# Half of the output mix by plain products, gate's residual moved into the feed-forward, embeddings split in two

## The chip, the core and the metric

The kernel runs on one core of a Trainium2 chip. The metric is the device time of one execution in microseconds (us), from runs without a profile. Its engines work side by side, each through its own list in order: TensorE (PE, matmuls; PEld loads its weights), VectorE (DVE), ScalarE (ACT), GpSimd (POOL) and SyncE (SP). SP, POOL and ACT also start DMA transfers, which all stand in that engine's list: a transfer that must wait holds what is behind it.

## The reference

One layer of a trunk with 512 tokens and 2048 channels, in float32:

```python
proj = h @ w_in                               # q, k, v of head groups A and B
oa   = banded_attention(qa, ka, va, ...)      # group A, windowed
ob   = dilated_attention(qb, kb, vb)          # group B, three dilations
ya, yb = rms_norm(oa, gn_a), rms_norm(ob, gn_b)
mix  = concatenate([ya, yb]) @ w_o
h    = layer_norm(ALPHA * h + mix, ln1_g, ln1_b)
ff   = square(relu(h @ w1)) @ w2              # 8192 wide
ple  = (p @ w_ple) * sigmoid(h @ w_ple_gate)  # per-layer embedding (256 wide) and its gate
h    = layer_norm(ALPHA * h + ff + ple, ln2_g, ln2_b)
```

## The kernel before

A float32 product is made of three matmuls of a reduced type: every operand is split in a high part (ScalarE, copy with rounding) and a low part (VectorE, the difference), and TensorE adds hi x hi, hi x lo and lo x hi. A weight tile is 128x1024 floats (512 KB); its parts are `wh` (L86) and `wl` (L87). `put` does the same for the other operand and makes the pair `s1h`, `s1l` and so on.

The large products use Strassen's scheme (`strassen`): over token halves (`th`) and quarters of the weight matrix, 7 products p of 4 steps k each take the place of 8. A step is 12 matmuls of 128x512, a call is 28 steps or 336 matmuls. The operands of the 7 products are sums of quarters: on the weight side VectorE makes them (L518, L523, L535, L536 and others), on the token side the `factors` (tiles `qh`, loaded from DRAM; in the feed-forward `qs`). Three PSUM chains `a`, `b`, `c` collect products; `quarters` puts them together to result quarters (th, nh) and hands each to a function: `mixed`, `gated`, `squared` or `last_sum`.

The stages, in order: input projection and attention (to about 500 us in the trace), with its last pieces between the embeddings `embed(0)` to `embed(3)` (48 matmuls for each two, p x w_ple, stored in `ple_d`); RMSNorm (`rms_stats`, `rms_scale`: the factor `r` by small VectorE ops L296 to L302, spread by TensorE L306, copied L322, applied L326, stored in `y_d`); the mix in two calls (`c` = 0, 1), each for half of the output columns; the first layer norm (`norm_rows`: rows L641, transposes `pt` L629, factors `ha`, stored in `h_d`, and `z_d` for the rows themselves); gate in two calls; eight chunks of the first feed-forward product (`squared`, factors stored in `s_d`); the second feed-forward product; the last layer norm. `gated` (L685 to L696) takes each quarter of gate: it loads the embedding `pl`, the normalized rows `zn` and LayerNorm's two rows `gb`, broadcast over all partitions, through ACT's list, and computes sig x ple + ALPHA x (zn x gain + bias), which goes to `z_d` as the residual for the last norm.

The program is written in this order of calls; a scheduler sorts the instructions of each engine by its own estimates, and tiles are drawn from rings (tags) with a fixed number of buffers: a new tile waits until the last reader of the buffer's former tile is done. Rings that matter here: "g" (4 buffers), "q" (2), "r" (4), "k" (4) and "wh", "wl" (3 each).

## Time and profile before

| | us |
|---|---|
| median of 3 runs (lowest, highest) | 2283.46 (2281.01, 2284.67) |
| the profiled execution | 2283.15 |
| its span, first to last instruction | 2281.4 |
| TensorE busy | 2156.5 (95%) |
| VectorE busy | 1663.9 (73%) |
| ScalarE busy | 1074.0 (47%) |

TensorE's mean granted clock is 0.977 of full speed. In the rows below, "L566" is a line of the kernel, "`b<-wh,s5h`" an instruction that writes tile `b` from `wh` and `s5h`, and a bracket at a row's end the idle time of the engine before it with what ended it. TensorE is busy nearly all the time, so the stretches in which it is not are what there is to read.

### The profile page before, as it was taken

To read this page: it belongs to the slowest core of one execution; us is meant where nothing else is said; L and a number is where in the kernel's file an instruction comes from. 1 tells how busy PE (TensorE), PEld (TensorE's weight loads), DVE (VectorE), ACT (ScalarE), POOL (GpSimd) and SP (SyncE) were. 2 spreads that over 40 slices of the span, in tenths; PEclk is the share of its full clock that TensorE was granted. 3 is DMA by queue.
4 is the path that set the end of the run, shared out by engine and by line. 5 is a ranking of instruction groups with operands and counts; after the bars stand their busy time and mean duration, and the time that the engine had idled before them with its cause. 6 is when DMAs were issued, how large, how long until landed. Compare 5 with 4: busy or idle time off the path is not lost.

```text
span 2281.4 us, 25611 instructions
## 1 busy us (share of the span) xinstructions
PE 2156.5 (95%) x9528; PEld 1743.6 (76%) x9528; DVE 1663.9 (73%) x1890; ACT 1074.0 (47%) x1300; POOL 112.9 (5%) x188
## 2 busy tenths in 40 slices
PE   8999999997997979899999999999899999999995
PEld 7888888875776757688887888877687787787784
DVE  7675655546988878777776876877777776777787
ACT  5454333344544634354554555455455455555331
POOL 0000000000001000000000000000011011101000
PEclk9999999998998989999999999999999999999998
DMA  6212322237767786655565565567669779679562
GB/s 226 77 65 83 114 72 83 78 105 282 245 203 244 268 260 204 196 205 197 197 231 171 189 231 174 195 231 249 191 197 267 192 202 278 176 216 285 170 242 102
DMA packets 132285, 433.01 MB, mean 190 GB/s; under 512 B 13600, under 2 KB 22832, under 8 KB 132160
## 3 DMA queue, kind: packets, MB, share of 16 engines
q1 hardware_dynamic: 93984, 300.19, 39.2%
q0 software_dynamic: 25760, 93.43, 14.3%
q10 hardware_dynamic: 12416, 37.75, 4.9%
q8 instruction: 75, 1.23, 0.2%
q14 instruction: 50, 0.41, 0.1%
HBM read 352.68 MB, written 78.64 MB: 189 GB/s over the span
## 4 chain that ended last, share of the span: by engine, by line
PE 71%; DMA 11%; DVE 11%; issue 4%; ACT 2%; DVEq 0%; SPq 0%; ACTq 0%
PE a L569 9%; PE a L566 9%; PE a L568 9%; PE u L93 6%; PE u L94 6%; PE u L95 6%; PE b L569 5%; PE b L568 5%; PE b L566 5%; DVE wl L87 4%; DMA wr<-in_w 3%; DMA qs<-s_d 2%; DMA gb<-in_lnb 2%; PE c L569 2%; PE c L566 2%
## 5 line engine op out<-in xcount | busy, mean ns | idle before, releaser
L86 ACT ACTIVATE wh<-wr 128x1024 fp32r<-128x1024 f32 (+1 forms) x400 | 415.3, 1042 | 562.0 <-PE a L568 222.1
L87 DVE TENSOR_TENSOR wl<-wr,wh 128x1024 fp32r<-128x1024 f32 (+1 forms) x400 | 477.4, 1198 | 223.3 <-ACT wh L86 218.5
L86 ACT ACTIVATE wh<-wk 128x1024 fp32r<-128x1024 f32 x160 | 169.6, 1060 | 201.7 <-PE a L568 99.1
L87 DVE TENSOR_TENSOR wl<-wk,wh 128x1024 fp32r<-128x1024 f32 x160 | 194.5, 1220 | 67.8 <-ACT wh L86 67.1
L93 PE MATMUL u<-xh,wh 128*128 128x512 f32 x576 | 227.6, 395 | 5.9 <-ACT xh L73 5.9
L95 PE MATMUL u<-xh,wl 128*128 128x512 f32 x576 | 226.0, 392 | 0.0
L94 PE MATMUL u<-xl,wh 128*128 128x512 f32 x576 | 225.5, 391 | 0.0
L518 DVE TENSOR_TENSOR wk<-wr,wk 128x1024 f32<-128x1024 f32 x80 | 97.8, 1223 | 91.0 <-DMA wr<-in_w 86.8
L566 PE MATMUL b<-wh,s5h 128*128 128x512 f32 x320 | 130.5, 408 | 24.6 <-ACT wh L86 13.6
L569 PE MATMUL b<-wl,s5h 128*128 128x512 f32 x320 | 130.6, 408 | 12.9 <-DVE wl L87 12.9
L569 PE MATMUL c<-wl,s2h 128*128 128x512 f32 x320 | 128.4, 401 | 9.8 <-DVE wl L87 9.7
L569 PE MATMUL a<-wl,s1h 128*128 128x512 f32 x320 | 128.9, 403 | 8.2 <-DVE wl L87 8.2
L566 PE MATMUL a<-wh,s1h 128*128 128x512 f32 x320 | 128.3, 401 | 4.5 <-ACT wh L86 2.3
L568 PE MATMUL b<-wh,s5l 128*128 128x512 f32 x320 | 129.8, 406 | 1.9 <-DVE s5l L445 1.9
L569 PE MATMUL a<-wl,s7h 128*128 128x512 f32 x320 | 126.8, 396 | 4.0 <-DVE wl L87 4.0
L566 PE MATMUL a<-wh,s7h 128*128 128x512 f32 x320 | 127.0, 397 | 3.2 <-ACT wh L86 1.7
L93 PEld LDWEIGHTS u<-xh,wh 128*128 128x128 f32 x576 | 108.7, 189 | 27.6 <-ACT xh L73 5.9
L569 PE MATMUL b<-wl,s3h 128*128 128x512 f32 x320 | 126.7, 396 | 2.5 <-DVE wl L87 2.4
L566 PE MATMUL a<-wh,s6h 128*128 128x512 f32 x320 | 125.5, 392 | 3.2 <-DVE zl L743 2.1
L566 PE MATMUL c<-wh,s2h 128*128 128x512 f32 x320 | 127.8, 399 | 0.0
L568 PE MATMUL c<-wh,s2l 128*128 128x512 f32 x320 | 127.6, 399 | 0.0
L568 PE MATMUL b<-wh,s3l 128*128 128x512 f32 x320 | 127.4, 398 | 0.0
(234 smaller groups left out, 4548.7 us busy)
## 6 DMA issues: line engine op xcount, KB each, us to landing
wr<-in_w SPq DMA_DIRECT2D x196, 512.0 KB, 4.0
wr<-in_w_in SPq DMA_DIRECT2D x64, 512.0 KB, 3.8
wq<-in_w SPq DMA_DIRECT2D x64, 512.0 KB, 3.9
wk<-in_w POOLq DMA_DIRECT2D x64, 512.0 KB, 4.8
qs<-s_d SPq DMA_DIRECT2D x56, 512.0 KB, 4.9
z_d<-ev POOLq DMA_DIRECT2D x42, 512.0 KB, 7.2
s_d<-f POOLq DMA_DIRECT2D x32, 512.0 KB, 5.2
wg<-in_w SPq DMA_DIRECT2D x32, 512.0 KB, 4.7
```

Of the source, the lines that this page charges most:

```text
L86: nc.scalar.activation(hi, t, AF.Copy)
L87: nc.vector.tensor_tensor(lo, t, hi.bitcast(F32), op=ALU.subtract)
L93: nc.tensor.matmul(o, wh, ah, start=start, stop=False)
L94: nc.tensor.matmul(o, wh, al, start=False, stop=False)
L95: nc.tensor.matmul(o, wl, ah, start=False, stop=stop)
L518: nc.vector.tensor_tensor(t4[k], get(b21, k, 2, "r"), t2[k], op=ALU.subtract)
L566: nc.tensor.matmul(o, sh[:, i, x], wh[:, c], start=first and k == 0 and j == 0, stop=False, skip_group_check=skip)
L568: nc.tensor.matmul(o, sl[:, i, x], wh[:, c], start=False, stop=False, skip_group_check=skip)
L569: nc.tensor.matmul(o, sh[:, i, x], wl[:, c], start=False, stop=k == 3 and j == 1, skip_group_check=skip)
```

## The change

Three edits go together, and their places in the order of the instructions follow below.

1. Half 0 of the mix is made by `plain`, an ordinary product of 4 pieces of 96 matmuls (384 instead of 336), on the unsummed factors `s1`, `s7` (blocks 0 and 2; the second is stored under the key 21), `s2`, `s4`. The first piece needs head group A alone and is interleaved with attention's end; the second needs group B. The sums that half 1 still needs are made meanwhile (`y_sums`). The PSUM pool of attention is split in two sides so that four banks live on.
2. `embed(2)` and `embed(3)` come after the mix; the split embedding input `ph`, `pl` is loaded and made again in buffers of `s1l`, results go through ring "q".
3. `gated` keeps the sigmoid and stores it in `g_d`. The rest (`residual`) is spread over the eight chunks of the first feed-forward product, a quarter in each: loads by SP in step 7 of 28, scaling in the 11th, sums and a store by POOL in the 14th.

```diff
-    embed(0)
-    V = v_split(V)
-    embed(1)
-    hd.turn()
-    embed(2)
-    ssB = hd.values(V, ssB, oB)
-    rB = rms_stats(ssB)
-    embed(3)
-    rms_scale(oB, rB, 8)
+    for g in range(2):
+        put(sy[g], 1, y_block(g, 0))
+        put(sy[g], 7, y_block(g, 2), 21)
+    embed(0, p_hl, bank, "g")
+    V = v_split(V)
+    embed(1, p_hl, bank, "g")
+    hd.turn()
+    o = [bank() for _ in range(NQ)]
+    plain(0, 0, o, range(2))
+    ssB = hd.values(V, ssB, oB)
+    plain(0, 0, o, range(2, 3))
+    rB = rms_stats(ssB)
+    plain(0, 0, o, range(3, 4))
+    rms_scale(oB, rB, 8)
...
+    for g in range(2):
+        put(sy[g], 2, y_block(g, 1))
+        put(sy[g], 4, y_block(g, 3))
...
+    def plain(nh, kh, o, steps=range(4)):
+        for k in steps:
+            wh, wl = w_split(w_load(w_o[0, 2 * kh + nh, k], "r"))
+            for j in range(2):
+                i = 2 * (k % 2) + j
+                c = slice(j * S, (j + 1) * S)
+                for t in range(NQ):
+                    ah, al = sy[k // 2][((1, 2), (21, 4))[t // 2][kh]]
+                    x = slice((t % 2) * P, (t % 2 + 1) * P)
+                    first, end = kh == k == j == 0, kh == j == 1 and k == 3
+                    nc.tensor.matmul(o[t], ah[:, i, x], wh[:, c], start=first, stop=False)
+                    nc.tensor.matmul(o[t], al[:, i, x], wh[:, c], start=False, stop=False)
+                    nc.tensor.matmul(o[t], ah[:, i, x], wl[:, c], start=False, stop=end)
...
+    plain(0, 1, o, range(2))
+    y_sums(0)
+    plain(0, 1, o, range(2, 4))
+    y_sums(1)
+    plain_out(0, o)
...
+    plain(1, 0, o)
+    for g in range(2):
+        x, y = y_block(g, 0), y_block(g, 2)
+        nc.vector.tensor_tensor(x, x, y, op=ALU.subtract)
+        put(sy[g], 7, x)
+    plain(1, 1, o)
+    plain_out(1, o)
...
-    for c in range(2):
-        def mixed(th, nh, y, c=c):
...
-            if c == 1 and all((th, m) in zs for m in range(4)):
-                norm_rows(th)
-        strassen(lambda k, q, c=c: w_o[c, q, k], sy, quarters(mixed, {(1, 0): "k"} if c else {}),
-                 between=mid if c == 0 else {}, steps=ENDS if c else FIRST1)
+    def mixed(th, nh, y):
...
+        if (th, 5 - n) in zs:
+            norm_rows(th)
+            if th == 1:
+                ph, pl = (s_tile(f"p{c}", "s1l", (P, 2, S), R32) for c in "hl")
+                r = pair("pr", "q")
+                nc.sync.dma_start(r, pT.rearrange("k p s -> p k s"))
+                nc.scalar.activation(ph, r, AF.Copy)
+                nc.vector.tensor_tensor(pl, r, ph.bitcast(F32), op=ALU.subtract)
+                rest.append([(ph[:, k], pl[:, k]) for k in range(2)])
+
+    strassen(lambda k, q: w_o[1, q, k], sy, quarters(mixed, {(1, 0): "k"}), steps=ENDS)
+    for g in range(2, 4):
+        embed(g, rest[0], pt_bank, "q")
...
         def gated(th, nh, g, c=c):
-            n = 2 * c + nh
-            e = pair("pl", "g")
-            nc.scalar.dma_start(e, ple_d[th, n])
-            z = pair("zn", "g")
-            nc.scalar.dma_start(z, z_d[th, n])
-            gb = pair("gb", "g")
-            nc.scalar.dma_start(gb, bass.AP(tensor=lnb.tensor, offset=lnb.offset + n * S, ap=[[0, P], [D, 2], [1, S]]))
             nc.scalar.activation(g, g, AF.Sigmoid)
-            nc.vector.tensor_tensor(g, g, e, op=ALU.mult)
-            for i in range(2):
-                nc.vector.scalar_tensor_tensor(z[:, i], z[:, i], ALPHA, gb[:, 0], op0=ALU.mult, op1=ALU.mult)
-                nc.vector.scalar_tensor_tensor(z[:, i], gb[:, 1], ALPHA, z[:, i], op0=ALU.mult, op1=ALU.add)
-            nc.vector.tensor_tensor(g, g, z, op=ALU.add)
-            nc.scalar.dma_start(z_d[th, n], g)
+            nc.scalar.dma_start(g_d[th, 2 * c + nh], g)
...
+    def residual(th, n):
+        t = {}
+        def load():
+            for name, d in (("zn", z_d), ("sg", g_d), ("pl", ple_d)):
+                t[name] = pair(name, "g")
+                nc.sync.dma_start(t[name], d[th, n])
+            t["gb"] = pair("gb", "g")
+            nc.sync.dma_start(t["gb"], bass.AP(tensor=lnb.tensor, offset=lnb.offset + n * S,
+                                               ap=[[0, P], [D, 2], [1, S]]))
...
     for n in range(NFC):
+        mid = dict(at[False]) if n == NFC - 1 else {}
+        for i, step in zip((6, 10, 13), residual(n % 2, n // 2)):
+            mid[i] = mid.get(i, []) + [step]
```

The names below are the program's, "waits" names the queue or engine whose semaphore is waited for, and lines of the changed kernel are those of its own text. TensorE at the end of attention, before: the last embedding's matmuls (`u`), the spread of RMSNorm's factor (`s`), and the mix's first matmul:

```order
2352 L93 MATMUL u<-wh,ph 128x512
2353 L94 MATMUL u<-wl,ph 128x512
2354 L95 MATMUL u<-wh,pl 128x512
2355 L306 MATMUL s<-ident,r 128x128 [waits DVE_49,PE_49]
2356 L306 MATMUL s<-ident,r 128x128 x3
2357 L566 MATMUL a<-wh,s1h 128x512 [waits Activation_49]
```

The same place now: the end of the plain product over head group A (`s7`, L458 to L460), the spread, and the plain product over group B (`s2`):

```order
2405 L458 MATMUL u<-wh,s7h 128x512
2406 L459 MATMUL u<-wh,s7l 128x512
2407 L460 MATMUL u<-wl,s7h 128x512
2408 L307 MATMUL s<-ident,r 128x128 [waits DVE_49,PE_49]
2409 L307 MATMUL s<-ident,r 128x128 x3
2410 L458 MATMUL u<-wh,s2h 128x512 [waits DMAHW3_49,DMAHW2_49,DMAHW4_49,DMAHW1_49,DMAHW5_49,DMAHW0_49,DMAHW6_49,DMASW3_49,DMAHW7_49,PE_49,Activation_49]
2411 L458 MATMUL u<-wh,s2h 128x512
```

The embedding's matmuls in front of the spread have gone, and 96 matmuls of the mix stand there; behind it comes work that needs group B from DRAM, where before it was group A's.

VectorE in the norm, before: the rows of token half 1 (L641), the last quarter's residual (L666) with its statistics, and between them weight sums for gate's first product (L535, L536):

```order
714 L641 TENSOR_SCALAR xt<-xt,mv,r_5541 128x512 x2
715 L641 TENSOR_SCALAR c_5279<-c_5279,mv,r_5541 128x512 x2
716 L666 SCALAR_TENSOR_TENSOR c_5329<-xt,c_5329 128x1024 [waits DMAHW0_49]
717 L535 TENSOR_TENSOR wq<-wq,wr 128x1024 [waits DMAHW4_49,DMAHW2_49]
718 L594 BN_STATS bs_4446<-c_5329 128x6 [waits DVE_49]
719 L594 BN_STATS bs_4447<-c_5329 128x6
720 L599 BN_AGGR mv<-bs_4446 128x2 [waits DVE_49]
721 L536 TENSOR_TENSOR wk<-wk,wq 128x1024 [waits DMASW6_49]
```

VectorE after embeddings 2 and 3 now: `s1l` of both groups, which waits for TensorE, token factors from `h_d` (`qh`, L565 and L566), and gate's weight sums (L617, L618):

```order
725 L434 TENSOR_TENSOR s1l<-ha,s1h 128x1024 [waits PE_49] x2
726 L434 TENSOR_TENSOR s7l<-qh,s7h 128x1024 [waits Activation_49]
727 L434 TENSOR_TENSOR s4l<-qh,s4h 128x1024 [waits DMASW1_49,Activation_49]
728 L617 TENSOR_TENSOR wq<-wq,wr 128x1024 [waits DMAHW6_49,DMAHW2_49,DMAHW0_49]
729 L565 TENSOR_TENSOR qh<-qh 128x1024 [waits DMAHW7_49,DMAHW5_49]
730 L618 TENSOR_TENSOR wk<-wk,wq 128x1024 [waits DMASW0_49,DVE_49]
731 L88 TENSOR_TENSOR wl<-wq,wh 128x1024 [waits Activation_49]
732 L566 TENSOR_TENSOR qh<-qh 128x1024 [waits DVE_49]
733 L617 TENSOR_TENSOR wq<-wq,wr 128x1024 [waits DMAHW4_49,DMAHW3_49,DMAHW1_49]
734 L434 TENSOR_TENSOR s4l<-qh,s4h 128x1024 [waits DMASW3_49]
735 L618 TENSOR_TENSOR wk<-wk,wq 128x1024 [waits DVE_49]
736 L88 TENSOR_TENSOR wl<-wq,wh 128x1024 [waits Activation_49]
```

The weight sums that stood among the norm's rows stand behind the embeddings now, with the factors of gate's later products between them.

SyncE in the first feed-forward product now, in chunk 1 (before, only weights stand in this place):

```order
246 L80 DMA wq<-in_w 128x1024 [waits DMAHW7_49,DVE_49]
247 L752 DMA zn<-z_d 128x1024 [waits DMAHW0_49,DMASW0_49,DMAHW1_49,DVE_49,Activation_49]
248 L752 DMA sg<-g_d 128x1024 [waits DMAHW2_49,DMASW2_49]
249 L752 DMA pl<-ple_d 128x1024 [waits DMAHW3_49,DMASW3_49,DVE_49]
250 L754 DMA gb<-in_lnb 128x2x512 [waits DMAHW4_49,DMASW4_49]
251 L80 DMA wq<-in_w 128x1024 [waits DMAHW5_49,DVE_49]
252 L80 DMA wr<-in_w 128x1024 [waits DMAHW6_49,Activation_49]
253 L80 DMA wq<-in_w 128x1024 [waits DMAHW7_49,DVE_49]
254 L80 DMA wr<-in_w 128x1024 [waits DVE_49]
```

The four loads of the residual stand between weights; `zn`, `sg`, `pl` and `gb` each wait for a store of the chunk before (queues of GpSimd, "DMASW").

## Rows read from the trace of the kernel before

**Rows 1.** The page's first line.

```profile
span 2281.4 us, 25611 instructions
```

**Rows 2.** Windows: stretch, length, busy us (instructions) of each engine, granted clock, DMA share, GB/s.

```profile
638.00:717.00 79.00, 78.28 (x338) 62.79 (x336) 67.45 (x72) 33.17 (x32) 1.59 (x3) 1.00 0.65 213
717.00:760.00 43.00, 27.20 (x113) 20.17 (x114) 39.67 (x63) 28.10 (x46) 9.44 (x17) 0.74 0.80 289
830.00:922.00 92.00, 79.57 (x326) 62.97 (x326) 73.08 (x72) 37.39 (x36) 2.12 (x4) 0.93 0.71 228
922.00:1017.00 95.00, 86.82 (x370) 69.64 (x370) 70.13 (x64) 41.25 (x44) 2.12 (x4) 0.95 0.56 187
1017.00:1098.00 81.00, 81.00 (x369) 66.03 (x368) 59.86 (x52) 41.41 (x44) 4.27 (x8) 1.00 0.60 201
540.00:560.00 20.00, 13.07 (x49) 10.27 (x48) 16.65 (x18) 7.70 (x9) 2.17 (x4) 0.84 0.94 333
1030.00:1040.00 10.00, 10.00 (x46) 8.29 (x45) 10.00 (x10) 5.32 (x6) 0.00 (x0) 1.00 0.79 279
1040.00:1050.00 10.00, 10.00 (x46) 8.28 (x45) 5.16 (x5) 5.01 (x5) 0.00 (x0) 1.00 0.15 39
```

**Rows 3.** TensorE's timeline, attention's end: start, us, line, idle before.

```profile
531.51 0.39 PE L95 MATMUL u<-wh,pl 128*128 128x512 f32 x1
...
537.99 2.05 PE L306 MATMUL s<-ident,r 128*128 128x128 f32 x8 [6.10 <-DVE r L302]
...
542.25 0.79 PE L566 MATMUL a<-wh,s1h 128*128 128x512 f32 x1 [2.21 <-ACT rb L322]
```

**Rows 4.** Chain of waits, 532 to 562 and 580 to 600: start, us, what.

```profile
543.63 4.65 DVE o L326 x7
...
548.84 9.27 DMA qh<-y_d
...
585.43 5.69 DMA qh<-y_d
```

**Rows 5.** TensorE's timeline, the norm's first transposes (`pt`).

```profile
721.28 2.00 PE L629 MATMUL pt<-ident,xt 128*128 128x128 f32 x8 [4.43 <-DVE xt L641]
...
729.11 0.65 PE L629 MATMUL pt<-ident,c 128*128 128x128 f32 x4 [0.26 <-ACT ha L632]
```

**Rows 6.** TensorE's waits, 765 to 1020: us in total, times, longest.

```profile
PE b L569 <- DVE wl L87: 11.5, 3, 5.8
PE a L569 <- DVE wl L87: 6.0, 1, 6.0
PE c L569 <- DVE wl L87: 4.9, 3, 2.4
```

**Rows 7.** VectorE's lines, 765 to 1017: count, busy, mean ns, idle before.

```profile
L693 DVE SCALAR_TENSOR_TENSOR zn<-zn,gb 128x512 f32<-128x512 f32 x16 | 10.5, 687 | 22.9 <-DMA gb<-in_lnb 22.9
...
L691 DVE TENSOR_TENSOR c<-c,pl 128x1024 f32<-128x1024 f32 x8 | 9.7, 1218 | 0.0
```

**Rows 8.** VectorE's timeline: the norm, gate's half 1, chunk 7.

```profile
726.61 1.27 DVE L594 BATCH_NORM_STATS2 bs<-c 128x6 f32<-128x512 f32 x2
...
731.28 0.16 DVE L302 SCALAR_TENSOR_TENSOR r<-rt,r 128x2 f32<-128x2 f32 x1
...
855.68 3.49 DVE L87 TENSOR_TENSOR wl<-wr,wh 128x1024 fp32r<-128x1024 f32 x3
...
1524.15 1.23 DVE L535 TENSOR_TENSOR wr<-wq,wr 128x1024 f32<-128x1024 f32 x1 [3.52 <-DMA wq<-in_w]
```

**Rows 9.** DMA issues, 717 to 762: queue, count, KB, median us to landing.

```profile
h_d<-ha POOLq DMA_DIRECT2D x8, 512.0 KB, 3.8
...
qh<-h_d SPq DMA_DIRECT2D x5, 512.0 KB, 5.8
...
wq<-in_w_gate SPq DMA_DIRECT2D x3, 512.0 KB, 5.8
```

**Rows 10.** DMA issues of the page's section 6.

```profile
s_d<-f POOLq DMA_DIRECT2D x32, 512.0 KB, 5.2
```

More of the change, by code (lines that the diff above doesn't have):

```diff
@@ L393, in block_kernel, with embed @@
     hd.scores(q, k)
-    p_hl = []
-    for k in range(2):
-        r = t_f("pr", "q")
-        nc.sync.dma_start(r, pT[k])
-        p_hl.append(split(r, "p", "q"))
-    def embed(g):
+    g_d = dr.tile([2, 4, P, 2, S], F32, name="g_d")
+    def embed(g, p, bank, tag):
         wh, wl = w_split(w_load(w_ple[g], "r"))
         for th in range(2):
-            e = pair("pe", "g")
+            e = pair("pe", tag)
             for i in range(2):
@@ new lines, in block_kernel, with x_load, plain_out @@
+    zs = {}
+    def x_load(th, n, z):
+        nc.scalar.dma_start(z, xn[th * HS:(th + 1) * HS, n * S:(n + 1) * S].rearrange("(t p) s -> p t s", p=P))
+    def plain_out(nh, o):
+        for th in range(2):
+            zs[th, nh] = z = pair("xt", "g")
+            x_load(th, nh, z)
+            for i in range(2):
+                nc.vector.scalar_tensor_tensor(z[:, i], z[:, i], ALPHA, o[2 * th + i], op0=ALU.mult, op1=ALU.add)
+            take_stats(th, nh, z)
+    bs = [st.tile([P, 4, nc.vector.BN_STATS_DIM], F32, name=f"bs{t}", bufs=1) for t in range(NQ)]
@@ new lines, in take_stats, with row_stats @@
+    def take_stats(th, n, z):
+        for i in range(2):
+            nc.vector.bn_stats(bs[2 * th + i][:, n], z[:, i])
+    def row_stats(th):
+        mv = st.tile([P, 2, nc.vector.BN_AGGR_DIM], F32, name="mv")
+        for i in range(2):
+            nc.vector.bn_aggr(mv[:, i], bs[2 * th + i])
+        v = st.tile([P, 2], F32, name="v2")
+        nc.vector.tensor_scalar(v, mv[:, :, 1], LN_EPS, None, op0=ALU.add)
+        r = st.tile([P, 2], F32, name="r2")
+        rsqrt(r, v)
+        return mv, r
@@ new lines, in block_kernel, with y_sums @@
+    sb = sbc.__enter__()
+    ps["c"] = ps["pt"] = ctx.enter_context(tc.tile_pool(name="pc", bufs=1, space=bass.MemoryType.PSUM, side="right"))
+    for g in range(2):
+        put(sy[g], 2, y_block(g, 1))
+        put(sy[g], 4, y_block(g, 3))
+    def y_sums(g):
+        x = y_block(g, 3)
+        nc.vector.tensor_tensor(x, x, y_block(g, 2), op=ALU.add)
+        put(sy[g], 5, x)
+        nc.vector.tensor_tensor(x, x, y_block(g, 0), op=ALU.subtract)
+        put(sy[g], 6, x)
+        y = y_block(g, 1)
+        nc.vector.tensor_tensor(y, y, x, op=ALU.subtract)
+        put(sy[g], 3, y)
@@ new lines, in block_kernel, with chain, pt_bank @@
+    plain(0, 1, o, range(2))
[3 more added lines that the diff above has]
+    plain_out(0, o)
+    pus.__exit__(None, None, None)
+    ps["a"] = ps["b"] = ctx.enter_context(tc.tile_pool(name="pa", bufs=1, space=bass.MemoryType.PSUM))
+    def chain(c):
+        return ps[c].tile([P, 2, S], F32, name=c, tag=c, bufs=1)
+    def pt_bank(shape=(P, S)):
+        return ps["pt"].tile(list(shape), F32, name="pt", tag="pt", bufs=2)
+    o = chain("c")
+    o = [o[:, 0], o[:, 1], pt_bank(), pt_bank()]
@@ L455, in get @@
                 q[i] = block("qh")
-                load(i, q[i])
-        def a1():
-            get(0)
-            put(sg, 1, q[0])
-        def a2():
-            get(2, 3)
-            nc.vector.tensor_tensor(q[3], q[3], q[2], op=ALU.add)
-            put(sg, 5, q[3])
-        def a3():
-            get(0)
-            nc.vector.tensor_tensor(q[3], q[3], q[0], op=ALU.subtract)
-            put(sg, 6, q[3])
-        def b1():
-            get(1)
-            put(sg, 2, q[1])
+                nc.sync.dma_start(q[i], h_d[g, i])
         def b2():
@@ L503, in strassen @@
     def strassen(src, sg, read, hold=False, between={}, steps=None):
-        bank = {c: ps.tile([P, 2, S], F32, name=c, tag=c, bufs=1) for c in "abc"}
+        bank = {c: chain(c) for c in "abc"}
         b11, b12, b21, b22, t1, t2, t3, t4 = ({} for _ in range(8))
@@ L553, in strassen @@
                 f()
-            chain, first = CHAIN[p]
+            ch, first = CHAIN[p]
             wh, wl = w_split(factor(p, k))
@@ L571, in strassen @@
             if k == 3:
-                read(p, bank[chain])
+                read(p, bank[ch])
     def quarters(done, tags={}):
@@ L625, in turned @@
         for b0 in (0, 2):
-            pt = ps.tile([P, 2, HS], F32, name="pt", tag="pt", bufs=2)
+            pt = pt_bank((P, 2, HS))
             for b in range(2):
@@ L729, in squared @@
                 keep(3, f[0, 1])
-        strassen(lambda k, q, n=n: w1[n, q, k], sh, quarters(squared), between=at[False] if n == NFC - 1 else {})
+        strassen(lambda k, q, n=n: w1[n, q, k], sh, quarters(squared), between=mid)
     gb = []
```

98 lines of the change are left out of this document (47 added, 51 removed).

## The prediction

> **What bounds the kernel now.** First the span and the time around it [rows 1]: the profiled execution took 2283.15 us, 1.75 us more than its span. Then the windows from one product to the next [rows 2]: TensorE's 128x512 matmul costs 78.28 / 338 = 0.2316 us in a row without gaps, so a product of 336 matmuls is 77.8 us, and 81.0 us in a feed-forward chunk, which also holds 32 transposes (3.2 us). Against this three stretches are long: half 0 of the mix, which starts at 542.25 [rows 3] and ends at 638, and gate's half 1 with the first feed-forward chunk (92 and 95 us). Between them the norm takes 43 us for 48 matmuls and 64 transposes, at a granted clock of 0.74. Everything later runs at 81 us a chunk; the change leaves it alone but for the new residual work.
>
> Then the waits of each long stretch. At attention's end TensorE waits 6.10 us for RMSNorm's factor and 2.21 us for its copy `rb` [rows 3]. Head group B is scaled after that (4.65 us for seven of eight ops), goes to memory and comes back; the load that closes this chain takes 9.27 us [rows 4], while the DMA engines are 94% busy (540 to 560 in [rows 2]). In the norm it waits 4.43 us for the first normalized rows [rows 5]. From gate's half 1 to chunk 0 TensorE waits for `wl`, the low half of a weight tile, seven times, 22.4 us together and 6.0 at the longest [rows 6], and the cause is one line: VectorE stands 22.9 us in front of L693, for the two broadcast rows `gb` [rows 7]. It works in order, so the weights' splits queue behind. L693 and L694 take 10.5 us each in these stretches, L691 and L695 9.7 each, 40.4 us together (one of each pair stands in [rows 7]).
>
> **The change, part by part.** Its price is made against the profiled execution, by stretch.
>
> 1. *Attention's end and half 0.* Before, the last embedding matmul starts at 531.51 [rows 3]. 48 embedding matmuls leave (11.1 us) and the first 96 plain ones come in (22.2), so TensorE is busy to about 542.6, and the spread of RMSNorm's factor (2.05) ends at 544.7 where it ended at 540.0; the 6.10 us are covered. `rb` follows at once, 545.4 at its end, because the puts that held ScalarE are earlier now. From `rb`'s end (542.25) to the load's issue (548.84) is 6.6 us [rows 3, 4], so B's load starts at 552.0. Its duration is an unknown with both ends in the trace: 5.69 and 9.27 us [rows 4]; I take the middle, 7.5. With the put on ScalarE (1.05) the plain product over B starts at 560.5, after about 16 us without work: the wait is one and long instead of several and short. Then 288 matmuls, 66.7 us. I add 2.5 us for a `wl` that stands behind the factor sums on VectorE (bounds 0 and 6.0, the longest such wait [rows 6]), and 1.5 us for a low clock after the wait (the granted clock of 540 to 560 is 0.84 [rows 2]). Half 1 starts at 631.2 instead of 638: -6.8.
>
> On this load, the rows have 9.27 us with the engines 94% busy [rows 2, 4]. The Trainium skill (DMA: Bandwidth & Descriptors, Issuing engines are not separate DMA queues) says that transfers started from several engines run on the same 16 DMA engines and interleave, so GpSimd's prefetched weights take their share of it; its row agrees. By that rule alone the long end would hold, and half 1 would start 1.8 us later.
>
> 2. *Half 1 of the mix.* 77.8 us, the 32 transposes of token half 1, which now stand before the last 17 matmuls instead of behind them (3.2 us, as in a chunk [rows 2]), and 0.9 us for the rows they wait for: 81.9 instead of 79, +2.9.
>
> 3. *Norm, embeddings 2 and 3, gate's first product.* From the last matmul: VectorE needs seven full-tile ops before the first normalized rows (sum, residual, sum of halves, two `s5l`, two `wl`), at 3.49 / 3 = 1.16 us each in a row, 8.1; four row statistics and the first two rows, all half tiles, at 1.27 a pair, 3.8; 14 small ops, one after the other, at some 0.19 each (0.16 and the gap), 2.6 [rows 8]: 14.5. Transposes with ScalarE's copies as they went before, 721.28 to 729.8 [rows 5]: 8.5. Embeddings: 48 matmuls 11.1, and 1.5 for two PSUM banks that ScalarE must empty between them: 12.6, to 35.6 us after the mix. Behind it VectorE has the `s1l` of both groups, which wait for the last embedding matmul because `ph` and `pl` hold their buffers, and then the sums for gate's first product, which were done during the mix's tail and the norm before. From `s1l` to the split that gate's next product needs I count 21 full-tile ops: 24.4 us. The first weight's load waits for embedding 3's store to leave ring "q", and behind it lie the `h_d` loads; store 2.7 at best, or 3.8 as `h_d`'s, load 5.8 [rows 9]. Against VectorE's queue this is some 2 us late, and the third and fourth weights, asked for when the first two are split, 4 us together. 35.6 + 24.4 + 6 = 66 us instead of 43: +23. The bounds: 56 (the embeddings run inside those first 14 us and the loads are not late) and 82 (each of the four weights comes 4 us late).
>
> 4. *Gate and chunk 0 without the residual.* Gate's half 0 has 288 matmuls left, 66.7, and 0.5: 67.2 instead of 70, -2.8. Half 1: 77.8 + 0.4 instead of 92, -13.8. Chunk 0: 81 as its neighbour, -14. VectorE's stall at `gb` is gone from here, and what is late next is nothing that I find: of the 73 us that it worked in half 1 [rows 2] four quarters' residuals, 4 x 5.2 = 21, leave, so 52 of 78 remain.
>
> 5. *The residual in the feed-forward chunks.* Per chunk VectorE gets 1.22 + 4 x 0.69 + 1.22 = 5.2 us [rows 7], SyncE four loads, GpSimd one store. In before's chunk VectorE is full to 1040, 23 us in, and busy for 5.16 of the next 10 us [rows 2]; the new work is scaled at the 11th of 28 steps and summed at the 14th, there. SyncE's `gb` waits for the last `s_d` store of the chunk before, whose buffers it takes (ring "g", issue to landing 5.2 us [rows 10]); the weights behind it are for steps 13 and later, so chunks 1 to 6 cost 1.0 us together (bounds 0 and 12, two a chunk). Chunk 7 differs: there a `wq` that VectorE needs for the fifth step, and already waited 3.52 us for [rows 8], now stands behind the four loads on SyncE: +2.5 (0 to 8).
>
> Sum: -6.8 + 2.9 + 23 - 2.8 - 13.8 - 14 + 1.0 + 2.5 = -8.0. 2283.15 - 8.0 = 2275.2; the median shown is 0.3 us above the profiled execution, so 2275.5.
>
> **Rivals.**
>
> *A, the norm hides the embeddings.* For it: of the 43 us TensorE works 27 [rows 2], and the embeddings need no normalized row. Against: the instruction order puts them behind the transposes. The stage takes 56 us: 2265.5.
>
> *B, gate's first product is held (the other side).* Place: ring "q" and the two `s1l`. Each of the four weights needs a buffer freed by an embedding store or a split, then a load of 5.8 us, and VectorE sums only then. For it: the DMA engines are 80% busy in the norm [rows 2], a weight's load took 5.8 us there [rows 9]. At 82 us the kernel takes 2291.5. It decides from 66 + 12.5 = 78.5 us, where the whole is slower than the median by 0.2%.
>
> *C, the residual is not hidden in the chunks.* SyncE waits at `gb`, VectorE at the residual, 1 to 2 us in each of seven chunks, about 9: 2284.5, no change. For it: gate shows what a `gb` that lands late does. Against: the idle share of 1040 to 1050.
>
> *D, the gate does not gain what it waits.* If the DMA engines rather than this helper's queue were behind the late `wl`, half 1 and chunk 0 keep half of their excess, 14 us: 2289.5. Against: 22.9 us at one line.
>
> **How the numbers follow.** 0.2%, 4.6 us, is about what a measurement can tell from no change; the bounds are 2278.9 and 2288.0. My forecast has 0.48 (its own range 2269 to 2281: B's load, the `wl`, a few us of the norm), A 0.14, B 0.15, C 0.14, D 0.09. Faster: 0.40 of the forecast's 0.48 and A, 0.54. Same: the rest of the forecast, 0.08, most of C, 0.12, and a part of B and D, 0.05: 0.25. Slower: 0.21. The range 2263 to 2291 leaves out the far ends of A and of B.
>
> **What would show it.** Right: one idle of 13 to 18 us before the first matmul of the plain product over `s2h`; half 1 of the mix starting at 629 to 634; gate's product `a` 63 to 70 us after the mix's last matmul; no VectorE wait for `gb` over 3 us before the feed-forward, and 78 and 81 us for gate's half 1 and chunk 0; chunks 1 to 6 at 81 to 82 us. Wrong: a first weight of gate that lands over 50 us after the mix, chunks at 83 or more, or `wl` waits of 5 us left in gate's half 1.

## The result, and the profile after

The changed kernel takes 2304.58 us (median of 4 runs, 2297.35 to 2308.33) against 2284.07 (4 runs, 2281.01 to 2286.66) of the kernel before on the same chip: a ratio of 1.0087, 95% interval 1.0059 to 1.0114. It is slower by 0.9%, where 2275.5 us (0.35% less than before) was forecast, and outside the forecast's range. The profiled execution took 2308.33 us, 25.2 more than that of before.

```profile
span 2306.6 us, 25695 instructions
```

The windows of after, with the columns of [rows 2]: half 1 of the mix, the norm with the embeddings, gate's half 1, chunk 0, chunks 1 to 6 of the first feed-forward product, chunk 7.

```profile
637.00:718.00 81.00, 80.86 (x366) 65.01 (x365) 62.28 (x76) 40.97 (x49) 6.76 (x12) 1.00 0.63 215
718.00:794.00 76.00, 38.19 (x135) 27.22 (x135) 58.20 (x69) 32.44 (x45) 4.64 (x8) 0.71 0.66 230
...
860.00:938.00 78.00, 77.43 (x337) 62.84 (x336) 59.74 (x53) 37.30 (x37) 2.65 (x5) 1.00 0.66 219
938.00:1018.00 80.00, 79.86 (x360) 65.15 (x359) 56.21 (x49) 40.17 (x42) 2.12 (x4) 1.00 0.56 183
1018.00:1524.00 506.00, 493.94 (x2209) 401.96 (x2208) 385.29 (x343) 248.83 (x264) 28.72 (x54) 0.99 0.66 225
1524.00:1624.00 100.00, 86.53 (x370) 67.97 (x369) 74.63 (x67) 50.54 (x55) 4.79 (x9) 0.93 0.73 247
```

The same stretches of before that [rows 2] don't hold, chunks 1 to 6 and chunk 7:

```profile
1017.00:1507.00 490.00, 487.16 (x2208) 396.72 (x2207) 359.46 (x307) 248.52 (x264) 25.63 (x48) 1.00 0.59 200
1507.00:1599.00 92.00, 86.07 (x373) 67.20 (x372) 70.97 (x61) 51.17 (x56) 4.27 (x8) 0.98 0.70 241
```

Gate's half 1 and chunk 0 shrink from 92 and 95 us to 78 and 80, and the seven waits for `wl` of [rows 6] are gone. The norm grows from 43 to 72 (718.5 to gate's first `a` matmul at 790.7), chunks 1 to 6 from 490 to 506, chunk 7 from 92 to 100. In chunks 1 to 6 TensorE is busy 6.8 us more for the same matmuls: its granted clock is 0.99 instead of 1.00, since four of its six waits there, those of 2.2 to 2.6 us, are followed by some us at the lower of its two levels (0.53 in the mean from 1076.5 to 1080.1). The rest is idle time.

In the norm of after two waits are 27 us of it (TensorE's waits, 718 to 800: us in total, times, longest):

```profile
PE pt L685 <- DVE xt L697: 15.7, 1, 15.7
PE b L648 <- ACT wh L87: 11.5, 1, 11.5
```

What stands behind the second, and behind the weight after it, is seen in the chain of waits (start, us, what):

```profile
766.57 6.18 DMA ple_d<-pe
772.77 3.41 DMA wq<-in_w_gate
...
790.74 0.50 PE a L648
```

An embedding result must reach memory before its buffer of ring "q" can take a weight of gate: gate's first `wq` starts at 766.90, when the third result has landed, the next at 772.77, when the last one has. At attention's end TensorE has one wait of 19.81 us before the plain product over group B (TensorE's timeline, then the DMA issues of 545 to 567: count, KB, median us to landing):

```profile
566.74 1.22 PE L458 MATMUL u<-wh,s2h 128*128 128x512 f32 x2 [19.81 <-ACT s2h L433]
```

```profile
wk<-in_w_o POOLq DMA_DIRECT2D x4, 512.0 KB, 7.3
qh<-y_d SPq DMA_DIRECT2D x4, 512.0 KB, 11.0
```

The loads of B took 11.0 us in the median, more than both of [rows 4], and four weights that GpSimd starts land beside them. But these are not what is new: before, GpSimd started four there as well (the same lines of before, 545 to 560):

```profile
wk<-in_w_o POOLq DMA_DIRECT2D x4, 512.0 KB, 7.0
qh<-y_d SPq DMA_DIRECT2D x4, 512.0 KB, 9.7
```

In a chunk, last, there is a small wait of TensorE for the transposes (`pt`), 0.9 to 2.6 us, which ends with VectorE's sum `c` (TensorE's waits, after from 1018 to 1524, then before from 1017 to 1507):

```profile
PE pt L786 <- DVE c L666: 12.1, 6, 2.6
```

```profile
PE pt L711 <- DVE c L584: 2.8, 3, 1.8
```

VectorE, which makes what the transposes need, waits more for weights that come from memory and less for their high part `wh`, which ScalarE makes (VectorE's waits, 1018 to 1524):

```profile
DVE wl L88 <- ACT wh L87: 61.1, 38, 2.9
DVE wk L600 <- DMA wr<-in_w: 40.4, 24, 3.2
...
DVE zn L761 <- DMA gb<-in_lnb: 6.4, 6, 2.1
```

Before, in chunks 1 to 6, these were 90.8 us for `wh`, time in which VectorE was ahead, and 25.3 for `wr`:

```profile
DVE wl L87 <- ACT wh L86: 90.8, 70, 1.6
DVE wk L518 <- DMA wr<-in_w: 25.3, 22, 2.5
```

### The profile page after: what moved, and what is told of

The parts are those of the page before. It is cut to its first block, busy times and chain, and to the rows that moved or that the text cites. A ratio compares the mean times of both kernels' runs of the same rounds, so it can differ in the third digit from the quotient of the medians.

```text
span 2306.6 us, 25695 instructions
## 1 busy us (share of the span) xinstructions
PE 2162.6 (94%) x9576; PEld 1753.4 (76%) x9576; DVE 1633.1 (71%) x1864; ACT 1061.5 (46%) x1287; POOL 115.1 (5%) x192
## 4 chain that ended last, share of the span: by engine, by line
PE 61%; DMA 14%; DVE 11%; issue 11%; ACT 2%; POOL 0%; DVEq 0%; SPq 0%; ACTq 0%; POOLq 0%
DMA wr<-in_w 7%; PE a L651 7%; PE a L648 7%; PE a L650 7%; PE u L94 6%; PE u L96 6%; PE u L95 6%; DVE wl L88 5%; PE b L648 3%; PE b L651 3%; PE b L650 3%; PE c L651 2%; PE c L648 2%; PE c L650 2%; DMA qs<-s_d 2%
## 5 line engine op out<-in xcount | busy, mean ns | idle before, releaser
L87 ACT ACTIVATE wh<-wk 128x1024 fp32r<-128x1024 f32 x152 | 161.0, 1060 | 189.4 <-PE a L650 93.5
L88 DVE TENSOR_TENSOR wl<-wk,wh 128x1024 fp32r<-128x1024 f32 x152 | 184.9, 1220 | 61.4 <-ACT wh L87 61.2
L648 PE MATMUL b<-wh,s5h 128*128 128x512 f32 x304 | 121.9, 401 | 31.6 <-ACT wh L87 31.6
L96 PEld LDWEIGHTS u<-xh,wl 128*128 128x128 f32 x576 | 108.7, 189 | 22.9
L95 PEld LDWEIGHTS u<-xl,wh 128*128 128x128 f32 x576 | 108.9, 189 | 22.4 <-DVE xl L75 0.4
L651 PE MATMUL b<-wl,s5h 128*128 128x512 f32 x304 | 121.5, 400 | 3.3 <-DVE wl L88 3.3
L651 PE MATMUL c<-wl,s2h 128*128 128x512 f32 x304 | 121.1, 398 | 3.6 <-DVE wl L88 3.3
L651 PE MATMUL a<-wl,s1h 128*128 128x512 f32 x304 | 120.2, 395 | 1.4 <-DVE wl L88 1.4
L648 PE MATMUL a<-wh,s4h 128*128 128x512 f32 x304 | 120.5, 396 | 0.9 <-DVE c L666 0.6
L650 PE MATMUL a<-wh,s7l 128*128 128x512 f32 x304 | 121.2, 399 | 0.0
```

Source lines behind the costliest of these rows:

```text
L87: nc.scalar.activation(hi, t, AF.Copy)
L88: nc.vector.tensor_tensor(lo, t, hi.bitcast(F32), op=ALU.subtract)
L95: nc.tensor.matmul(o, wh, al, start=False, stop=False)
L96: nc.tensor.matmul(o, wl, ah, start=False, stop=stop)
L648: nc.tensor.matmul(o, sh[:, i, x], wh[:, c], start=first and k == 0 and j == 0, stop=False, skip_group_check=skip)
L650: nc.tensor.matmul(o, sl[:, i, x], wh[:, c], start=False, stop=False, skip_group_check=skip)
```

## The experiments

Each ratio is to the kernel before on the same chip at the same time (its median lay between 2280.7 and 2284.2). 0.1% is 2.3 us. Lengths of chunks come from one profiled execution of each run.

### Which of the three edits costs, which gains

**Gate's residual back in gate** (the changed kernel without edit 3).

```diff
         def gated(th, nh, g, c=c):
+            ...the residual's loads and sums, as before
-            nc.scalar.dma_start(g_d[th, 2 * c + nh], g)
...
-        for i, step in zip((6, 10, 13), residual(n % 2, n // 2)):
-            mid[i] = mid.get(i, []) + [step]
```

> The changed kernel with gate's residual back in gate, so the feed-forward chunks carry none of it. Theory: the chunks lose time because VectorE's 5.2 us of residual delay the weights' chain there, and gate's half 1 and chunk 0 gained 29 us because VectorE no longer stood at gb. Then chunks 1 to 6 go from a mean of 84.4 back to 81 to 82 us, chunk 7 from 99.8 to 91 to 93, while gate's half 1 and chunk 0 go back from 78 and 80 to about 92 and 95: 2304 - 15 - 8 + 29, about 2310 us. Rival: the chunks are slow for something earlier (weights that start late, a shifted prefetch): they stay at 84, and the kernel takes about 2330.

Measured: 2311.87 us, 1.0132 (1.0115 to 1.0150). Gate's half 1 and chunk 0 are back at 92.2 and 97.9 us, chunks 1 to 6 at 489.9, chunk 7 at 90.3. So edit 3 gains about 10 us in the changed kernel (1.0132 to 1.0087), and the other two cost 30. The total is the 2310 us expected; that VectorE's 5.2 us are the chunks' loss, as the expectation has it, is not shown by this run.

**Only edit 3, in the kernel before.**

```diff
-            n = 2 * c + nh
-            ...loads of pl, zn, gb
             nc.scalar.activation(g, g, AF.Sigmoid)
-            ...sums
-            nc.scalar.dma_start(z_d[th, n], g)
+            nc.scalar.dma_start(g_d[th, 2 * c + nh], g)
...
+        for i, step in zip((6, 10, 13), residual(n % 2, n // 2)):
+            mid[i] = mid.get(i, []) + [step]
```

> The kernel before with the residual's move alone. Theory: gate's half 1 78 and chunk 0 80 us (29 us gained), chunks 1 to 6 at 84 and chunk 7 at 99 (23 us lost), mix, embeddings and norm as before: about 2278 us. Rival: the chunks' loss comes only together with the other two parts: about 2256.

Measured: 2267.12 us, 0.9941 (0.9924 to 0.9958): faster than both kernels, midway between the two expectations. Chunks 1 to 6 take 500.2, chunk 7 97.9; the profiled execution was the shortest of the six, 5 us under their median.

**Edits 1 and 3, the embeddings not behind the mix** (all four at attention's end, 2 and 3 while B's load is on its way).

```diff
     rms_scale(oB, rB, 8)
+    for g in range(2, 4):
+        embed(g, p_hl, lambda: bank("s"), "g")
...
-    for g in range(2, 4):
-        embed(g, rest[0], pt_bank, "q")
```

> The changed kernel with embeddings 2 and 3 behind the scaling of group B, where TensorE stood idle for 19.8 us until group B came back from DRAM, and no longer after the mix. Theory: there they cost TensorE nothing, the idle shrinks to about 8 us, and gate's product a follows the mix's last matmul after 43 to 48 us again instead of 72 to 75: about 2304 - 28 = 2276 us. Rival: their weights, stores and PSUM copies stand in front of group B's load and its factors, so half 1 of the mix starts 8 to 11 us later: about 2286.

Measured: 2270.25, 0.9946 (0.9927 to 0.9965). Against the changed kernel's 1.0087 that is 1.41%, 32 us, for the place of two embeddings and for their ring, which is "g" here and "q" there.

**Edit 1 alone** (embeddings as in the last run, gate's residual back).

> The changed kernel with gate's residual back in gate and embeddings 2 and 3 in the wait for group B: what is left of the change is half 0 by plain products. Theory: half 1 of the mix starts about where it started before (638, perhaps 636), gate and the chunks are as before: about 2282 us, no change. Rival: the plain half itself costs time that the embeddings' place hid: over 2290.

Measured: 2287.36, 1.0024 (1.0010 to 1.0038): half 0 by plain products costs some 5 us and gains nothing that can be seen, again between the two expectations.

**Embeddings behind the mix, results in ring "g"** instead of "q".

```diff
-        embed(g, rest[0], pt_bank, "q")
+        embed(g, rest[0], pt_bank, "g")
```

> The changed kernel with the results of embeddings 2 and 3 in ring g instead of ring q; they stay after the mix. Theory: the norm's 75 us come from ring q, since gate's first weights wait for the embeddings' stores there and their sums stand behind; with ring g gate's first product runs in the norm's waits again, and product a follows the mix after 50 to 58 us: about 2304 - 20 = 2284 us. Rival: the stage is long for the embeddings' matmuls and VectorE's chain of the norm itself: 66 us or more, about 2297 or slower.

Measured: 2280.92, 0.9998 (0.9980 to 1.0016), 0.89% or 20 us less than the changed kernel by one letter, as the theory had it. SyncE's timeline in the changed kernel (740 to 780), and in this run (675 to 760):

```profile
741.16 24.16 SPq L556 DMA_DIRECT2D qh<-h_d  x8
766.90 0.33 SPq L80 DMA_DIRECT2D wq<-in_w_gate  x1
```

```profile
681.31 0.33 SPq L80 DMA_DIRECT2D wq<-in_w_gate  x1
...
684.09 0.33 SPq L80 DMA_DIRECT2D wq<-in_w_gate  x1
...
735.40 19.89 SPq L80 DMA_DIRECT2D wq<-in_w_gate  x2
```

The loads of `wq` for gate, of which the changed kernel starts none before 766.90, now start at 681.31, 684.09, 735.40 and 754.97, two of them under the mix, and gate's half 1 starts at 841.7 instead of 859.6. From the mix's last matmul to gate's `a` it is 53.5 us, instead of 72 with ring "q" and 43 before the change. So of the 29 us that this stage grew by, ring "q" made some 18; the other 11 come with the embeddings behind the mix.

### What the residual costs in the chunks

**No residual at all.**

```diff
-        for i, step in zip((6, 10, 13), residual(n % 2, n // 2)):
-            mid[i] = mid.get(i, []) + [step]
```

> The kernel before with gate's residual taken out of gate and put nowhere: sigmoid is stored, and neither the four loads nor the six operations nor the store of the sum are done (part of the computation is left out). It gives gate's gain by itself. If gate gains the 29 us that the other runs point to and the chunks stay as before: 2250 to 2256 us; the sums alone (2255.4) would then cost nothing and the loads all. If the sums cost 1 us a chunk of their own: 2244 to 2249 us.

Measured: 2248.67, 0.9861 (0.9843 to 0.9880). Gate's gain alone is 1.39%, 31.7 us, a little more than the 29 thought. The time lies in the second of the ranges expected, 2244 to 2249, that of sums which cost 1 us a chunk of their own; against it the moved residual (0.9941) costs 0.80%, 18.3 us. Chunks 1 to 6 take 489.8 us, chunk 7 90.6, as before the change. So the moved residual is what lengthens the chunks.

**Loads and store without VectorE's sums.**

```diff
         def scaled():
-            ...
+            pass
         def summed():
-            ...the sums
             nc.gpsimd.dma_start(z_d[th, n], t["zn"])
```

> The kernel before with the residual's move alone, but VectorE's six operations of the residual left out (the four loads by SyncE and the store by GpSimd stay; the residual itself is then missing from the output). Theory: VectorE's 5.2 us delay the chain split, load, sum of the weights in ring r, which was paced by its own length and had no slack; without them chunks 1 to 6 go from a mean of 83.4 (residual's move alone) back to 81.5 to 82 us and chunk 7 from 97.9 to about 94: about 2254 us. Rival: the loads on SyncE hold the weights behind them: chunks stay at 83 to 84, about 2265.

Measured: 2272.59, 0.9946 (0.9930 to 0.9961): 0.85%, 19.4 us over the run without any residual; chunks 1 to 6 take 506.7, chunk 7 98.8. Both expectations were lower. The theory that VectorE's sums are the whole loss fell.

**Sums and store without the loads** (the same six operations on tiles that are there anyway).

```diff
         def load():
-            ...four loads
+            pass
```

> The kernel before with the residual's move alone, but its four loads left out: VectorE does the same six operations on tiles that are in memory already (the residual is then wrong), and the store stays. Theory of VectorE's chain: chunks 1 to 6 stay at about 83, chunk 7 at 96 to 98: about 2265 us. Rival, SyncE's loads: chunks back to 81.5, chunk 7 to 92: about 2251. If both have a part, the loss divides between this run and the one without sums.

Measured: 2255.37, 0.9871 (0.9854 to 0.9887): 0.10%, 2.3 us over no residual, with an interval from some -3 to +8. The chunks say more: 1 to 6 take 497.2, as the theory of VectorE's chain had it, chunk 7 94.5, and the two profiled executions are 7.6 us apart. The four runs side by side (this one also takes one buffer of ring "g" in a chunk and not four; the store to `z_d`, which runs with either half, was not tried alone):

| in the chunks | ratio | chunks 1 to 6 | chunk 7 |
|---|---|---|---|
| nothing | 0.9861 | 489.8 | 90.6 |
| sums and store | 0.9871 | 497.2 | 94.5 |
| loads and store | 0.9946 | 506.7 | 98.8 |
| all | 0.9941 | 500.2 | 97.9 |

Each half alone lengthens the chunks, the loads more than the sums, and the two don't add up: the loads alone cost as much as all. The sums alone give TensorE the wait that the changed kernel has, and VectorE nearly the changed kernel's waits (TensorE's, then VectorE's, in chunks 1 to 6 with sums and store):

```profile
PE pt L729 <- DVE c L586: 8.0, 6, 2.3
```

```profile
DVE wl L87 <- ACT wh L86: 62.9, 47, 3.1
DVE wk L520 <- DMA wr<-in_w: 39.6, 23, 2.9
```

So the longer wait for `wr` in the changed kernel (40.4) comes about without any of the four loads: VectorE's six operations, with the store, are enough for it. VectorE's sum `c`, for which TensorE's transposes wait, starts in chunks 1 to 6 on average 54.3 us into a chunk with nothing, 55.3 with the sums, 55.8 with all and 57.2 with the loads. VectorE's waits in chunks 1 to 6 without any residual, and with the loads alone:

```profile
DVE wl L87 <- ACT wh L86: 90.7, 70, 1.6
DVE wk L520 <- DMA wr<-in_w: 28.0, 24, 2.3
```

```profile
DVE wl L87 <- ACT wh L86: 72.1, 54, 2.5
DVE wq L525 <- DMA wq<-in_w: 32.7, 18, 6.2
DVE wk L520 <- DMA wr<-in_w: 30.9, 23, 2.9
```

With the loads alone weights land late: VectorE waits for `wq` 32.7 us, where it was 1.7 without residual, and TensorE waits 9.1 us for `wl`. Where the transfers collide is in the busy share of the DMA engines, one digit (tenths) per us over the first 40 us of chunk 2 (chunk 3 in the run without residual). Before:

```profile
DMA  0075796599999899898618710000000376392573
```

Without any residual:

```profile
DMA  1066399799979999999834910000000166473376
```

The changed kernel:

```profile
DMA  2056699699999999999989999983100498986037
```

Stores of `f` and the refill of the weights' rings fill the engines from the 8th to the 20th us, and from the 24th to the 30th us nothing moves. The four residual loads and their 2 MB go into the full stretch; it lasts to the 26th us, and of the pause two us are left. The mean share of the stage, 0.59 and 0.66, shows nothing of this. With the sums and no loads the pause is whole, and the chunks are longer all the same; so the burst is behind the loads' part of the loss at most.

**The arithmetic on GpSimd.**

```diff
-            nc.vector.tensor_tensor(...)
+            nc.gpsimd.tensor_tensor(...)   # and so on, 7 operations for 6
```

> The kernel before with the residual's move alone, its arithmetic done by GpSimd instead of VectorE (seven operations, the same result). Theory of VectorE's chain: the chunks come back to 81.5 to 82 and chunk 7 to 92 to 95, about 2254 us. Rival: SyncE's loads remain, and GpSimd's weights and stores wait behind its arithmetic: chunks at 83 or more, 2265 or slower.

Measured: 2306.22, 1.0102 (1.0085 to 1.0119); chunks 1 to 6 take 532.0. The rival held, the theory didn't. VectorE's lines in them (count, busy, mean ns, idle before):

```profile
L87 DVE TENSOR_TENSOR wl<-wr,wh 128x1024 fp32r<-128x1024 f32 x96 | 124.5, 1302 | 40.7 <-ACT wh L86 40.4
L87 DVE TENSOR_TENSOR wl<-wk,wh 128x1024 fp32r<-128x1024 f32 x48 | 71.2, 1493 | 20.8 <-ACT wh L86 20.8
L87 DVE TENSOR_TENSOR wl<-wq,wh 128x1024 fp32r<-128x1024 f32 x24 | 40.3, 1678 | 0.0
```

With the sums on VectorE these were 1219, 1221 and 1218 ns: VectorE's own work was slower in the run in which GpSimd computes beside it. GpSimd needs 3.06 to 3.27 us for a 128x1024 sum, VectorE 1.22.

**The four loads started by GpSimd.**

```diff
-                nc.sync.dma_start(t[name], d[th, n])
+                nc.gpsimd.dma_start(t[name], d[th, n])   # gb too
```

> The kernel before with only gate's residual moved into the chunks (2267.1 us), but a chunk's four residual loads (zn, sg, pl, gb) are started by GpSimd instead of SyncE; VectorE's six operations and all transfers stay. Theory (the weights wq and wr stand behind the residual's loads in SyncE's queue, above all behind gb, which waits for a buffer of ring g): chunks 1 to 6 fall from 500.2 towards the 497.2 of the kernel without loads, chunk 7 from 97.9 towards 94.5, in all 2256 to 2261 us. Rival (it is the transfers themselves, 2 MB more at the DMA engines in the same 20 us, whoever starts them): 2265 to 2269 us. If GpSimd's wait for gb holds its weights wk later in the chunk: over 2270 us.

Measured: 2291.64, 1.0041 (1.0026 to 1.0057), chunks 1 to 6 531.3. SyncE was free of them, and against the same loads on SyncE (0.9941) it got worse by 23 us, which only the third expectation allowed; GpSimd's weights `wk`, which that one names, start 63 us into a chunk, long after `gb` at 20. GpSimd's timeline, the DMA issues of 1071 to 1110, and VectorE's timeline:

```profile
1082.43 0.53 POOL L698 DMA_DIRECT2D zn<-z_d  x1 [2.55 <-DMA s_d<-f]
```

```profile
wq<-in_w SPq DMA_DIRECT2D x4, 512.0 KB, 6.9
...
pl<-ple_d POOLq DMA_DIRECT2D x1, 512.0 KB, 11.3
```

```profile
1095.82 1.23 DVE L704 TENSOR_TENSOR sg<-sg,pl 128x1024 f32<-128x1024 f32 x1 [4.28 <-issue]
```

`pl`, started at 1084.42, is there 11.3 us later, when VectorE's 4.28 us of idle time end. The loads start when a store of `f` frees their buffer, 11.0 us into the chunk, as on SyncE; now SyncE's weights are started in the same us and not behind them, `pl` lands after 11.3 us (6.0 in the changed kernel), and VectorE's list stands with the weights' sums in it. The Trainium skill (DMA: Bandwidth & Descriptors, Issuing engines are not separate DMA queues) says that transfers started by several engines run on the same 16 DMA engines and interleave. The trace agrees, with 11.3 us for `pl`.

**The four loads started by ScalarE.**

```diff
-                nc.sync.dma_start(t[name], d[th, n])
+                nc.scalar.dma_start(t[name], d[th, n])   # gb too
```

> As the run with GpSimd, but ScalarE starts the four residual loads. Theory of the blocked queue: SyncE's weights come free as there, yet ScalarE itself now stands at gb's buffer and its wh conversions behind it, which the next weight factor needs: 2262 to 2275 us, over the run with GpSimd. Rival (transfers themselves): equal to the run with GpSimd, within 3 us.

Measured: 2310.24, 1.0125 (1.0108 to 1.0143), chunks 1 to 6 546.6, slower than both expectations. The blocked queue's cost is seen in ScalarE's timeline, a weight's conversion that stands behind a load that waits:

```profile
1085.44 1.06 ACT L86 ACTIVATE wh<-wr 128x1024 fp32r<-128x1024 f32 x1 [4.23 <-DMA s_d<-f]
```

**The product of sigmoid and embedding left in gate** (three loads and five sums a chunk).

```diff
+            nc.scalar.dma_start(e, ple_d[th, n])
             nc.scalar.activation(g, g, AF.Sigmoid)
+            nc.vector.tensor_tensor(g, g, e, op=ALU.mult)
```

> The kernel before with only gate's residual moved into the chunks (2267.1 us), but the product of sigmoid and embedding stays in gate: one load (pl, on ScalarE) and one VectorE operation per quarter there, and one load less on SyncE and one VectorE operation less in each chunk. Theory (loads ahead of weights plus sums): chunks 1 to 6 shorter by about a quarter of the 10 us loss, 497 to 498, chunk 7 by 1 to 2 us, gate's halves longer by 0 to 4 us: 2262 to 2267 us. Rival (it is gb's wait alone that matters): chunks unchanged, gate longer: 2267 to 2271 us.

Measured: 2267.73, 0.9933 (0.9917 to 0.9950), against 0.9941 with four loads: no difference that the intervals hold, so a loss in proportion to the bytes is not shown.

**The arithmetic three steps later**, loads on SyncE at step 6; with the loads on GpSimd; and with the product left in gate.

```diff
-        for i, step in zip((6, 10, 13), residual(n % 2, n // 2)):
+        for i, step in zip((6, 13, 16), residual(n % 2, n // 2)):
```

> The kernel before with only gate's residual moved into the chunks (2267.1 us), with its arithmetic at steps 13 and 16 of a chunk instead of 10 and 13; the loads stay on SyncE at step 6. Theory (VectorE, which takes its work in order, stands at the first residual operations until gb has landed, 5.4 us in six chunks, and the sums wl and wk behind them come late): that idle time goes and chunks 1 to 6 fall from 500.2 to 496 to 499, in all 2260 to 2265 us. Rival (SyncE's weights behind the four loads are the loss, whenever VectorE comes to the sums): 2265 to 2269 us.

> The four residual loads on GpSimd as in the run that took 2291.6 us, with the arithmetic at steps 13 and 16. Theory (there VectorE stood some 5 us in each chunk at the first product, whose data landed later because SyncE's weights, no longer held up, now streamed beside them): with six factors' more time before the first use the stall goes and what the freed SyncE gives remains: chunks 1 to 6 at 493 to 498 instead of 531, in all 2254 to 2262 us. Rival (GpSimd's transfers slow the weights themselves): still over 2270 us.

> The kernel before with gate's residual moved, the product of sigmoid and embedding kept in gate (2267.7 us) and the rest of the arithmetic at steps 13 and 16. Theory of VectorE's stand at gb: as the run with late arithmetic alone, less one load and one operation in a chunk: 2258 to 2264 us. Rival of the blocked SyncE: 2265 to 2268 us.

Measured: 2292.88, 1.0036 (1.0023 to 1.0049); 2288.88, 1.0012 (0.9998 to 1.0025); 2278.82, 0.9979 (0.9969 to 0.9989). The first and the third are 0.95% and 0.46% slower than their twins with early sums, the second 0.29% faster than its twin and nowhere near the 2254 to 2262 us expected. So the stand at `gb` is not shown to be the loss: the later sums cost more than they could save. The rivals' 2265 to 2269 us were missed as well; only that of the second run, over 2270, held. VectorE's timeline of the first of them:

```profile
1185.79 1.23 DVE L525 TENSOR_TENSOR wq<-wr,wq 128x1024 f32<-128x1024 f32 x1 [5.00 <-DMA wq<-in_w]
...
1188.07 1.22 DVE L704 TENSOR_TENSOR sg<-sg,pl 128x1024 f32<-128x1024 f32 x1
```

VectorE first stands 5.00 us at a late `wq`, and then does the residual while sums for TensorE are due. With the early sums the residual's work lies in that hole: there the wait for `wq` is 1.5 us in six chunks, here 38.5. With the same loads, sums three steps later cost 22 us: VectorE's steps are not equally free. At equal late sums the start by GpSimd is 0.24% better than by SyncE, 5 us; that this is SyncE's blocked list is likely, not shown.

**The loads at another step**: 10 (sums at 14 and 16), 12 (15 and 17), 2 (10 and 13).

```diff
-        for i, step in zip((6, 10, 13), residual(n % 2, n // 2)):
+        for i, step in zip((10, 14, 16), residual(n % 2, n // 2)):
```

> The kernel before with only gate's residual moved into the chunks (2267.1 us), with the four loads at step 10 of a chunk instead of 6 and the arithmetic at 14 and 16. Theory (the 16 DMA engines are nearly full in the first 24 us of a chunk, with the stores of f and the refill of the weights' rings, and idle from 24 to 31 us; the 2 MB of residual loads lengthen that burst and hold up the weights): from step 10 the loads start into the idle stretch, 2257 to 2264 us against the 2292.9 of late arithmetic with early loads. Rival (late arithmetic falls where VectorE is short, wherever the loads are): 2280 to 2295 us.

> As the run with the loads at step 10, with the loads at step 12 and the arithmetic at 15 and 17. Theory of the full DMA engines: within 4 us of that run, 2256 to 2266 us; over it by more only if the data land after VectorE's step 15. Rival (VectorE short there): 2280 to 2295 us.

> As the kernel before with only the residual moved (2267.1 us), with the loads at step 2 of a chunk instead of 6, arithmetic at 10 and 13 as there. Theory of the full DMA engines and of ring g (its four buffers come free as the stores of f land, about 12 to 18 us into the chunk): SyncE stands at the loads and the weights come later still, 2270 to 2290 us. Rival (the data of gb come too late for step 10, an earlier start helps): 2258 to 2265 us.

Measured: 2290.32, 1.0036 (1.0021 to 1.0050); 2292.45, 1.0047 (1.0030 to 1.0064); 2266.25, 0.9939 (0.9920 to 0.9955). The first two equal the run with late sums, the third the one with early sums, each outside what the burst's theory gave. The rival of the first two, that VectorE is short where late arithmetic falls (2280 to 2295), held in both. The trace says why they told nothing of the burst: `zn` starts 10.9 us into a chunk from step 10 and 11.2 from step 2, so the step moved no load. The expected pauses were not reached; a version whose loads do start in them was not tried.

## Why the prediction was wrong, by its steps

By the profiled executions the sum was to be -8.0 and is +25.2; the 33.2 us between are made up like this (from the start of one product to the next):

| step | predicted | measured | miss |
|---|---|---|---|
| 1: half 1 of the mix starts | -6.8 | -1.6 | +5.2 |
| 2, 3: half 1, norm, to gate's `a` | +25.9 | +32.7 | +6.8 |
| 4: gate's half 0 | -2.8 | -1.1 | +1.7 |
| 4: gate's half 1 | -13.8 | -14.1 | -0.3 |
| 4: chunk 0 | -14 | -14.8 | -0.8 |
| 5: chunks 1 to 6 | +1.0 | +15.8 | +14.8 |
| 5: chunk 7 | +2.5 | +8.5 | +6.0 |
| behind them | 0 | -0.2 | -0.2 |

**The step that failed is the fifth**, "the weights behind it are for steps 13 and later, so chunks 1 to 6 cost 1.0 us together", 20.8 of the 33.2 us, and outside its own bounds (12 and 8). It took VectorE's idle half of 1040 to 1050 in [rows 2] for room and the loads for a wait that holds only weights of steps 13 and later. Shown by runs: without the residual the chunks take 489.8 and 90.6 us, so that it is the moved residual that costs, 18 us when it is moved alone and some 24 by the stretches of the changed kernel. The loads alone cost 19.4 us. The sums, for which there was to be room, cost without the loads 2.3 us by the ratios and 11 by the chunks of the profiled executions. No other issuing engine and no later arithmetic mends it. Seen in the trace: the sum `c` that TensorE's transposes wait for is late by 1.0 us in a chunk with the sums alone, by 1.5 with all and by 2.8 with the loads alone, and with the loads the full stretch of the DMA engines grows by some 7 us. [rows 2] had a sign of that in two rows, a DMA share of 0.79 from 1030 to 1040 and 0.15 from 1040 to 1050; the step used only VectorE's column of the second. Not shown: how the 1.7 to 2.6 us a chunk divide between full DMA engines, SyncE's held list, the buffers of ring "g", the store and VectorE's list. Fewer bytes should have helped if the DMA engines alone were behind it, and one load less gave 0.08%, inside the interval.

**Step 4 was right.** By the run without residual, taking it out of gate gains 31.7 us, 30.6 predicted, and the waits for `wl` [rows 6] are gone. Rival D is out.

**Step 3 came near partly by luck:** 72 us where 66 was predicted. To the end of the embeddings it was 44.8 us, 9.2 more than the 35.6 of the sum (TensorE's transposes started 15.7 us after the mix, 14.5 predicted, and they and the embeddings took 29.1 instead of 21.1). Behind them it was 27.3 us, 3.1 less than predicted, but not by the term that the step put first. It gave 24.4 us to VectorE's queue of 21 operations and "some 2 us late" and 4 to the weights; VectorE had first to wait for gate's first weight, which landed 54 us after the mix (over 50 was named as a sign of being wrong), and ran nearly without a gap only then, for 18 us. With ring "g" much of this is done under the norm, and the kernel is 20 us faster. This is rival B's place and mechanism, at 72 us, below the 78.5 from which it was to decide.

**Step 1:** the load of B that TensorE waited for started at 554.8 us (552.0 predicted) and took 10.8 us, longer than the two bounds from [rows 4]; the long end, 9.27, came nearer than the 7.5 that the sum took. Why it was longer still is not shown: GpSimd's four `w_o` weights stood beside it before the change too. The wait before `s2h` is 19.8 us where 16 was predicted, and edit 1 alone costs 5 us.

**Rival C** was the nearest in kind, SyncE and VectorE held in each chunk, with half the price or less: "about 9" where it is 18 to 24.

## What to carry to other kernels

An engine's idle time in a stage that runs without gaps for TensorE need not be room: here six operations of VectorE, put where it was half idle, and four loads, put before a pause of the DMA engines, each lengthened the chunks alone. Price such work on every engine it uses us by us, not by the stage's mean share, and time its halves apart. Ask of every new tile whose ring it enters and what the next user of that buffer waits for; one ring's name was 20 us here. Edit 3 alone, 2267.1 us, beats the whole change and the kernel before, so edits that are put together are best timed apart.
